# A four-layer-step decoder trunk: gate weights of three column tiles split ahead, the second half's transposes at column tiles 5 to 8, and a PSUM bank of its own for the fourth product

## The chip, the core and the metric

The kernel runs on one core of one Trainium2 chip. The metric is the device time of one launch in microseconds (us). The core has a matrix engine (PE, TensorE), which multiplies a loaded 128x128 block by a moving operand of up to 512 columns and adds into PSUM; a vector engine (DVE); a scalar engine (ACT), used here for casts, copies and SiLU; POOL (GpSimd), which does elementwise work in SBUF and issues some DMAs; and SP (SyncE), which issues most DMAs. Every engine works through its own list of instructions in a fixed order, and waits at an instruction whose semaphores are not yet there; what stands behind it waits too. PSUM has eight banks of 512 float32 values per partition.

## The reference

The trunk has DEPTH = 2 layers; each layer is a feed-forward step, a mixer, and a second feed-forward step, all on x of 1024 rows by 1024 columns in float32. Only the feed-forward step is touched here:

```
def swiglu(x, wg, wu, wd):
    return (jax.nn.silu(x @ wg) * (x @ wu)) @ wd

f = swiglu(rmsnorm(h, ffn_pre_g), ffn_w_gate, ffn_w_up, ffn_w_down)   # D_FF = 1408
h = h + 0.5 * rmsnorm(f, ffn_post_g)
```

The mixer of layer 0 is differential attention beside gated linear attention; that of layer 1 is stick-breaking attention. There are four feed-forward steps, called here by layer and step: first (layer 0, f0), second (layer 0, f1), third (layer 1, f0), fourth (layer 1, f1). The second and the fourth follow a mixer; the third follows the second directly.

## The kernel before

**Precision.** Every operand of a matrix product is split into a rounded part (a cast on ACT) and the remainder (a subtraction on DVE, L337 for weights, L277 or L280 for the others); a product is three matmuls per 128 rows of the contraction (`mm3`, L287 to L289). A *quarter* is four such blocks, 12 matmuls of 512 columns, into one PSUM bank.

**The gate and up projections** (`gu`). The 1408 columns are NF = 11 column tiles of 128. The 1024 rows of x are two halves of 512. Two loops run over the tiles. The first loop computes the first half of the gate: per tile one quarter with the first four row blocks (first quarter) and, two tiles later, one with the other four into the same bank (second quarter, `a12`), with a copy of the bank in between (L434) and SiLU at the end (L414). In the same loop the second half of x is prepared: `second_half` transposes it on PE (L327), a pair of blocks in each of four column tiles, and `combos` makes from it on DVE and ACT the sums and differences of Strassen's scheme (L388 to L397, split by L276 and L277). The second loop then does seven products' worth of work as five quarters per tile: the first three into the banks pb, pc and pd; the fourth adds to pc and the fifth to pd. DVE reads the banks in between:

```
tt(out=c22, in0=pc, in1=u2, op=ALU.add)          # L472
tt(out=c22, in0=pd, in1=c22, op=ALU.add)         # L486
self.quarter(pc, w4, A22, False, True)           # fourth product, L488
tt(out=c21, in0=pc, in1=u2, op=ALU.add)          # L489
```

Weights come by SP as `rawt` tiles of 512 KB into four buffers of pool rp, and are split into six buffers of pool wp (two quarters per gate tile, so three tiles fill the pool). The up weights are first combined with the gate's on POOL (`blocks`, L421 to L424, four instructions a tile; t2 is the output of L422).

**The down projection** (`down_strassen`) has products da, db, dc, de and dd, each into four banks, from `ph` (the output of `gu`) and from rows of the down weights or sums of them, `rawd` tiles of 256 KB. After a half is done, `epilogue` adds it to the residual stream and normalizes it for the next step: DVE (L571, L232), a power on POOL (L234, the tile rs), DVE (L575 or L580), a square on ACT (L243), L232, L234 again, and the scaling on DVE (L248). The first half's rows are transposed on PE at once (`make_x`, L268). The second half's rows (tiles fo or xn) are those that `second_half` of the next step transposes.

**Order.** The instructions of an engine are put in order by a scheduler when the program is built; what goes through `pin` (keep_in_program_order) keeps its order against other pinned instructions of its engine. In the first loop the matmuls of the first tiles and all transposes are pinned on PE. The steps in `jobs` are DMAs that POOL issues: they copy and add blocks of weights in DRAM (the tiles vsum for the mixer's value weights, wsum for its output weights, dsum for the down weights), a few per column tile. The first feed-forward step also makes the masks of the mixer on POOL in this way. Before the end of a stage, `first_weights` already loads and splits the first weights of the next.

Of the kernel before, what the change touches and what calls it, by code (L numbers as in the profile page):

```python
# [19 lines left out]
P = 128  # L20
# [69 lines left out]
class Trunk:  # L90
# [263 lines left out]
    def gu(self, cx, wg, wu, A, xn1, gname, gi, jobs, begun):  # L354
# [45 lines left out]
        pin = self.tc.keep_in_program_order  # L400
        paces = 3, -(-len(jobs[1]) // NF)

        def job(loop):
            for f in jobs[loop][:paces[loop]]:
                f()
            del jobs[loop][:paces[loop]]

# [18 lines left out]

        for c in range(NF):

            self.pin_mm = pin if c < 6 else None
            h = [self.ph.tile([P, TB], F32, name="ph%d" % tb, tag="ph") for tb in range(2)]  # L430
            w0, w1 = begun if begun and c == 0 else self.gate_weights(wg, c)
# [3 lines left out]
            while len(second) > (c < 8):  # L435
                a12()
            second.append((ps, w1, h))
            ph.append(h)
            if 2 <= c <= 5:
                second_half(c - 2)  # L440
            if 4 <= c <= 7:
                combos(c - 4)
            if c > 2:
                job(0)
# [11 lines left out]
        for c in range(NF):  # L456
# [5 lines left out]
            pd = self.acc.tile([P, TB], F32, name="pd", tag="acc")  # L462
            if c == NF - 1:
                pe = self.acc.tile([P, TB], F32, name="pe", tag="acc")
                pf = self.acc.tile([P, TB], F32, name="pf", tag="acc")
# [19 lines left out]
            else:  # L485
                tt(out=c22, in0=pd, in1=c22, op=ALU.add)  # L486
                w4, w3 = self.split_w(B["t4"]), self.split_w(B["b22"])
                self.quarter(pc, w4, A22, False, True)  # L488
                tt(out=c21, in0=pc, in1=u2, op=ALU.add)  # L489
# [7 lines left out]
            job(1)  # L497
# [113 lines left out]
    def ffn(self, l, f, x0, xn1, hsrc, hdst, last):  # L611
# [8 lines left out]
        jobs = [], []  # L620
        if l + f == 0:
            jobs = self.mask_steps() + sums((self.value_blocks(0), self.tv)), sums(down, (self.out_blocks(0), self.td))
        elif l == 0:
            jobs = [], sums(down, (self.value_blocks(1), self.tv))
        elif f == 0:
            jobs = [], sums(down)
# [4 lines left out]
        r = self.down_strassen(wd, self.wd[l, f], ph, pg, hsrc, hdst, None if last else nxt)  # L631
# [19 lines left out]
    def down_strassen(self, w, T, ph, pg, hsrc, hdst, nxt):  # L651
# [994 lines left out]
    def build(self):  # L1646
# [14 lines left out]
        for h in x1:  # L1661
# [6 lines left out]
                  (lambda l=l, f=int(step[1]): self.gate_weights(a["ffn_w_gate"][l, f], 0)) for l, step in stages]  # L1668
# [43 lines left out]
```

## Time and profile before

| | |
|---|---|
| time, median of 3 runs | 2486.64 us (2486.34 to 2493.13) |
| profiled execution | 2488.17 us, span 2486.2 us |
| mean granted TensorE clock | 0.985 |
| PE busy | 2352.8 us, 95% of the span |
| DVE, ACT, POOL busy | 1840.1, 1141.2, 723.4 us |

The span runs from the first to the last instruction of the profiled execution; 1.97 us lie around it. In a row of the timeline stand start, duration, engine, line and operation, output and inputs, the count of instructions merged into it and, in square brackets, how long the engine was idle before it and what ended the wait. In a row of the windows stand the length of the stretch and, for each engine, its busy time. Line numbers are those of the kernel before. The feed-forward steps' first loops lie at about 17 to 90 us, 937 to 1016 us, 1285 to 1359 us and 2140 to 2217 us.

### The profile page before, as it was taken

To read this page: it belongs to the slowest core of one execution; us is meant where nothing else is said; L and a number is where in the kernel's file an instruction comes from. 1 tells how busy PE (TensorE), PEld (TensorE's weight loads), DVE (VectorE), ACT (ScalarE), POOL (GpSimd) and SP (SyncE) were. 2 spreads that over 40 slices of the span, in tenths; PEclk is the share of its full clock that TensorE was granted. 3 is DMA by queue.
4 is the path that set the end of the run, shared out by engine and by line. 5 is a ranking of instruction groups with operands and counts; after the bars stand their busy time and mean duration, and the time that the engine had idled before them with its cause. 6 is when DMAs were issued, how large, how long until landed. Compare 5 with 4: busy or idle time off the path is not lost. (4 is left out here: it accounts for less than half of the span.)

```text
span 2486.2 us, 31734 instructions
## 1 busy us (share of the span) xinstructions
PE 2352.8 (95%) x11165; PEld 1925.0 (77%) x11165; DVE 1840.1 (74%) x2877; ACT 1141.2 (46%) x2285; POOL 723.4 (29%) x729
## 2 busy tenths in 40 slices
PE   7999999999888898999989999999999999799998
PEld 6778877777677776877768878778888878588886
DVE  7768789387577778678688677785767677786777
ACT  6323456332466666423456225463333345652343
POOL 3547210011011111567022563110332430234520
PEclk9999999999999998999999999999999999899999
DMA  8867444411112463767454743355574244532234
GB/s 240 229 154 187 141 148 155 143 52 68 60 60 77 150 222 108 194 151 180 140 184 125 162 118 123 122 167 180 126 185 104 90 131 163 176 85 76 73 110 170
DMA packets 278407, 343.64 MB, mean 138 GB/s; under 512 B 13972, under 2 KB 190312, under 8 KB 277736
## 3 DMA queue, kind: packets, MB, share of 16 engines
q1 hardware_dynamic: 251352, 261.39, 33.6%
q0 software_dynamic: 26896, 80.22, 14.2%
q8 instruction: 88, 1.44, 0.2%
q14 instruction: 71, 0.58, 0.1%
HBM read 292.28 MB, written 124.78 MB: 168 GB/s over the span
## 5 line engine op out<-in xcount | busy, mean ns | idle before, releaser
L234 POOL TENSOR_TENSOR rs<-ms,nhalf 128x1 f32<-128x1 f32 (+1 forms) x136 | 103.7, 769 | 839.6 <-DVE ms L232 728.7
L336 ACT CAST wq<-rawt 128x512 fp32r<-128x512 f32 x264 | 163.3, 622 | 362.6 <-PE pc L289 181.9
L337 DVE TENSOR_TENSOR wq<-rawt,wq 128x512 fp32r<-128x512 f32 x264 | 246.5, 938 | 41.9 <-ACT wq L336 37.9
L276 ACT CAST hl<-rawd 128x512 fp32r<-128x512 f32 x212 | 130.7, 620 | 212.0 <-PE dc L289 63.9
L277 DVE TENSOR_TENSOR hl<-rawd,hl 128x512 fp32r<-128x512 f32 x212 | 155.4, 737 | 81.6 <-ACT hl L276 81.5
L287 PE MATMUL pps<-hl,wh 128*128 128x512 f32 x512 | 209.3, 409 | 1.4 <-ACT k L966 1.2
L288 PE MATMUL pps<-hl,wh 128*128 128x512 f32 x512 | 203.6, 398 | 0.0
L289 PE MATMUL pps<-hl,wl 128*128 128x512 f32 x512 | 202.9, 396 | 0.0
L421 POOL TENSOR_TENSOR rawt<-rawt 128x512 f32<-128x512 f32 x44 | 65.7, 1494 | 342.7 <-DMA rawt<-in_ffn_w_up_dram 287.0
L287 PE MATMUL pa<-hl,wq 128*128 128x512 f32 x352 | 143.1, 407 | 5.8 <-ACT wq L336 3.2
L289 PE MATMUL pa<-hl,wq 128*128 128x512 f32 x352 | 141.0, 401 | 8.1 <-DVE wq L337 8.1
L287 PE MATMUL pc<-hl,wq 128*128 128x512 f32 x336 | 133.0, 396 | 12.7 <-DVE c L472 11.8
L288 PE MATMUL pa<-hl,wq 128*128 128x512 f32 x352 | 140.5, 399 | 0.0
L289 PE MATMUL pc<-hl,wq 128*128 128x512 f32 x336 | 133.3, 397 | 0.0
L288 PE MATMUL pc<-hl,wq 128*128 128x512 f32 x336 | 133.3, 397 | 0.0
L288 PE MATMUL pd<-hl,wq 128*128 128x512 f32 x336 | 131.3, 391 | 0.0
L289 PE MATMUL pd<-hl,wq 128*128 128x512 f32 x336 | 131.2, 391 | 0.0
L287 PE MATMUL pd<-hl,wq 128*128 128x512 f32 x336 | 131.1, 390 | 0.0
L1076 DVE TENSOR_TENSOR_SCAN a<-a,zero 128x128 f32<-128x128 f32 (+3 forms) x64 | 90.2, 1409 | 46.5 <-POOL a L1073 46.2
L983 PE MATMUL z<-k,q 128*128 128x512 f32 (+2 forms) x480 | 113.6, 361 | 9.5 <-ACT k L966 4.3
L287 PEld LDWEIGHTS pps<-hl,wh 128*128 128x128 f32 x512 | 97.7, 191 | 21.5 <-ACT k L966 2.6
L289 PEld LDWEIGHTS pps<-hl,wl 128*128 128x128 f32 x512 | 97.5, 191 | 21.1
(359 smaller groups left out, 6642.0 us busy)
## 6 DMA issues: line engine op xcount, KB each, us to landing
rawt<-in_ffn_w_gate_dram SPq DMA_DIRECT2D x88, 512.0 KB, 4.0
dsum<-in_ffn_w_down_dram POOLq DMA_DIRECT2D x48, 640.0 KB, 8.0
rawt<-in_ffn_w_up_dram SPq DMA_DIRECT2D x44, 512.0 KB, 4.2
rawd<-dsum SPq DMA_DIRECT2D x80, 256.0 KB, 2.7
hres<-h SPq DMA_DIRECT2D x40, 512.0 KB, 2.7
h<-hres SPq DMA_DIRECT2D x40, 512.0 KB, 4.6
rawd<-in_ffn_w_down_dram SPq DMA_DIRECT2D x76, 256.0 KB, 2.7
dsum<-dsum POOLq DMA_DIRECT2D x16, 640.0 KB, 5.7
```

The source lines that it names most:

```text
L234: nc.gpsimd.tensor_tensor(out=rs, in0=ms, in1=self.nhalf.to_broadcast([P, n]) if n > 1 else self.nhalf, op=ALU.pow)
L276: nc.scalar.copy(out=t[:, 0], in_=src)
L277: nc.vector.tensor_tensor(out=t[:, 1], in0=src, in1=t[:, 0].bitcast(F32), op=ALU.subtract)
L287: pin(nc.tensor.matmul(ps, lhsT=ah, rhs=bh, start=first, stop=False, skip_group_check=more))
L288: pin(nc.tensor.matmul(ps, lhsT=ah, rhs=bl, start=False, stop=False, skip_group_check=more))
L289: pin(nc.tensor.matmul(ps, lhsT=al, rhs=bh, start=False, stop=last, skip_group_check=more))
L336: nc.scalar.copy(out=w[:, 0], in_=src)
L337: nc.vector.tensor_tensor(out=w[:, 1], in0=src, in1=w[:, 0].bitcast(F32), op=ALU.subtract)
L421: gt(out=b11, in0=b12, in1=b11, op=ALU.subtract)
L983: nc.tensor.matmul(z[:, :wide], lhsT=lhs[:, i * P:(i + 1) * P], rhs=rhs[:, c0:c0 + wide], start=j == 0, stop=j == len(passes) - 1 and not ...
L1076: nc.vector.tensor_tensor_scan(out=ra, data0=ra, data1=self.zero1.to_broadcast([P, n]), initial=1.0, op0=ALU.mult, op1=ALU.add)
```

## The change

Four things are changed together.

1. `first_weights` loads and splits the gate weights of three column tiles instead of one before the last epilogue of the stage before.
2. In the first loop of `gu`, `second_half` is called at the column tiles 5 to 8 (c = 4 to 7) instead of 3 to 6, `combos` at 6 to 9 (c = 5 to 8) instead of 5 to 8; matmuls are pinned up to c = 7; the second quarters stay two tiles behind up to c = 8.
3. In the second loop the fourth product has a bank of its own, pe, in every tile (before: in the last alone), and a new SBUF tile c23, so that L472's and L486's results are kept apart. The numbers of instructions are the same.
4. In the first feed-forward step, POOL's mask steps and the sums vsum leave the first loop of `gu` (three steps a tile) and stand in `down_strassen`, all at once, behind POOL's last subtraction of that function (L725).

```diff
@@ gu
-        paces = 3, -(-len(jobs[1]) // NF)
-        def job(loop):
-            for f in jobs[loop][:paces[loop]]:
-                f()
-            del jobs[loop][:paces[loop]]
+        pace = -(-len(jobs) // NF)
+        def job():
+            for f in jobs[:pace]:
+                f()
+            del jobs[:pace]
...
         for c in range(NF):
-            self.pin_mm = pin if c < 6 else None
+            self.pin_mm = pin if c < 8 else None
             h = [self.ph.tile([P, TB], F32, name="ph%d" % tb, tag="ph") for tb in range(2)]
-            w0, w1 = begun if begun and c == 0 else self.gate_weights(wg, c)
+            w0, w1 = begun.pop(0) if begun else self.gate_weights(wg, c)
             ps = self.acc.tile([P, TB], F32, name="pa", tag="acc")
             self.quarter(ps, w0, A[0:4], True, True)
             nc.scalar.copy(out=h[1], in_=ps)
-            while len(second) > (c < 8):
+            while len(second) > (c < 9):
                 a12()
             second.append((ps, w1, h))
             ph.append(h)
-            if 2 <= c <= 5:
-                second_half(c - 2)
             if 4 <= c <= 7:
-                combos(c - 4)
-            if c > 2:
-                job(0)
+                second_half(c - 4)
+            if 5 <= c <= 8:
+                combos(c - 5)
...
             pd = self.acc.tile([P, TB], F32, name="pd", tag="acc")
+            pe = self.acc.tile([P, TB], F32, name="pe", tag="acc")
             if c == NF - 1:
-                pe = self.acc.tile([P, TB], F32, name="pe", tag="acc")
                 pf = self.acc.tile([P, TB], F32, name="pf", tag="acc")
...
             else:
-                tt(out=c22, in0=pd, in1=c22, op=ALU.add)
+                v = c22
+                c22 = tm.tile([P, TB], F32, name="c23", tag="c23")
+                tt(out=c22, in0=pd, in1=v, op=ALU.add)
                 w4, w3 = self.split_w(B["t4"]), self.split_w(B["b22"])
-                self.quarter(pc, w4, A22, False, True)
-                tt(out=c21, in0=pc, in1=u2, op=ALU.add)
+                self.quarter(pe, w4, A22, True, True)
+                tt(out=c21, in0=pe, in1=v, op=ALU.add)
@@ ffn
         if l + f == 0:
-            jobs = self.mask_steps() + sums((self.value_blocks(0), self.tv)), sums(down, (self.out_blocks(0), self.td))
+            jobs = sums(down, (self.out_blocks(0), self.td))
+            steps = sums((self.value_blocks(0), self.tv)) + self.mask_steps()
@@ down_strassen
         for j in range(KH):
             gt(out=ph[j + KH][0], in0=ph[j][0], in1=ph[j + KH][0], op=ALU.subtract)
+        for f in steps:
+            f()
@@ build
-                  (lambda l=l, f=int(step[1]): self.gate_weights(a["ffn_w_gate"][l, f], 0)) for l, step in stages]
+                  (lambda l=l, f=int(step[1]): [self.gate_weights(a["ffn_w_gate"][l, f], c) for c in range(3)])
+                  for l, step in stages]
```

How the built order moves is shown at three places. The first is ACT at the start of the second feed-forward step, where the first half's gate begins and the second half's last epilogue still runs. COPY ph is the copy behind a first quarter, ACTIVATE ph the SiLU behind a second quarter, `junk,ss<-h` the square of a residual row block, and `xr<-xps` reads the first transposes. Before:

```order
L434 COPY ph_8550<-pa 128x512
L336 CAST wq<-rawt 128x512
L243 ACTIVATE junk,ss<-h 128x1024
L414 ACT_TABLE_LOAD
L414 ACTIVATE ph_8509<-pa 128x512
L243 ACTIVATE junk,ss<-h 128x1024
L336 CAST wq<-rawt 128x512
L243 ACTIVATE junk,ss<-h 128x1024 x2
L329 ACTIVATE xr<-xps,gcol 128x512 x2
```

With the change:

```order
L433 COPY ph_8578<-pa 128x512
L336 CAST wq<-rawt 128x512
L243 ACTIVATE junk,ss<-h 128x1024
L412 ACT_TABLE_LOAD
L412 ACTIVATE ph_8545<-pa 128x512
L243 ACTIVATE junk,ss<-h 128x1024
L433 COPY ph_8607<-pa 128x512
L243 ACTIVATE junk,ss<-h 128x1024
L412 ACTIVATE ph_8561<-pa 128x512
L243 ACTIVATE junk,ss<-h 128x1024
```

Behind these follow three casts, the copy of the fifth tile, a cast, the third SiLU and then the first L329: the transposes now stand behind eight quarters instead of four, and the last square behind the second SiLU.

The second place is DVE between the second and the third feed-forward step, where the second half's sums (L757, L700), the weight splits (L337) and the epilogue (L571, L232, L580) stand in one list. Before:

```order
L757 TENSOR_TENSOR fo_3_11254<-dd_10862,u_10226 128x512
L700 TENSOR_TENSOR fo_2_11249<-fo_2_11249,pg 128x512
L337 TENSOR_TENSOR wq<-rawt,wq 128x512
L280 SCALAR_TENSOR_TENSOR hl<-xps,gcol,hl 128x512
L700 TENSOR_TENSOR fo_3_11254<-fo_3_11254,pg 128x512
L571 TENSOR_TENSOR s_11275<-fs_10221 128x1
```

With the change:

```order
L761 TENSOR_TENSOR fo_3_11294<-dd_10902,u_10266 128x512
L702 TENSOR_TENSOR fo_2_11289<-fo_2_11289,pg 128x512
L337 TENSOR_TENSOR wq<-rawt,wq 128x512
L280 SCALAR_TENSOR_TENSOR hl<-xps,gcol,hl 128x512
L702 TENSOR_TENSOR fo_3_11294<-fo_3_11294,pg 128x512
L337 TENSOR_TENSOR wq<-rawt,wq 128x512 x4
L571 TENSOR_TENSOR s_11331<-fs_10261 128x1
```

The splits of the second and the third tile (four) stand ahead of the epilogue; before, they stood one by one among its instructions.

The third place is POOL in the down projection of the first feed-forward step. With the change:

```order
L727 TENSOR_TENSOR ph_746<-ph_428,ph_746 128x512
L82 DMA vsum_132<-in_hyb_w_in_dram 256x512 x2
L82 DMA vsum_134<-in_hyb_w_in_dram 256x512 x2
L82 DMA vsum_132<-in_hyb_w_in_dram 256x512 x2
L82 DMA vsum_134<-in_hyb_w_in_dram 256x512 x2
L82 DMA vsum_133<-vsum_132 16x8192 x2
L82 DMA vsum_133<-in_hyb_w_in_dram 256x512 x2
L82 DMA vsum_135<-vsum_133 16x8192 x2
L82 DMA vsum_135<-in_hyb_w_in_dram 256x512 x2
L168 MEMSET zero_2427 128x1
```

After this MEMSET come 24 more mask instructions, and then the epilogue's powers (L234, 16 of them). Before, L234 stood directly behind L725, and all of these stood ahead of the first loop's and the second loop's L421 to L424.

More of the change, by code (lines that the diff above doesn't have):

```diff
@@ L399, in gu @@
         ph, second = [], []
-        pin = self.tc.keep_in_program_order
-        paces = 3, -(-len(jobs[1]) // NF)
-        def job(loop):
-            for f in jobs[loop][:paces[loop]]:
+        pace = -(-len(jobs) // NF)
+        def job():
+            for f in jobs[:pace]:
                 f()
-            del jobs[loop][:paces[loop]]
+            del jobs[:pace]
         def a12():
@@ L425, in blocks @@
             return {"t1": b11, "t2": t2, "t3": b12, "t4": b21, "b22": b22}
+        pin = self.tc.keep_in_program_order
         for c in range(NF):
-            self.pin_mm = pin if c < 6 else None
+            self.pin_mm = pin if c < 8 else None
             h = [self.ph.tile([P, TB], F32, name="ph%d" % tb, tag="ph") for tb in range(2)]
-            w0, w1 = begun if begun and c == 0 else self.gate_weights(wg, c)
+            w0, w1 = begun.pop(0) if begun else self.gate_weights(wg, c)
             ps = self.acc.tile([P, TB], F32, name="pa", tag="acc")
@@ L496, in gu @@
                 self.down_sums(ph, c - 1 - NF // 2)
-            job(1)
+            job()
         tmp.close()
@@ L619, in ffn @@
         down = self.down_blocks(l, f), self.wd[l, f]
-        jobs = [], []
+        jobs, steps = [], []
         if l + f == 0:
-            jobs = self.mask_steps() + sums((self.value_blocks(0), self.tv)), sums(down, (self.out_blocks(0), self.td))
+            jobs = sums(down, (self.out_blocks(0), self.td))
+            steps = sums((self.value_blocks(0), self.tv)) + self.mask_steps()
         elif l == 0:
-            jobs = [], sums(down, (self.value_blocks(1), self.tv))
+            jobs = sums(down, (self.value_blocks(1), self.tv))
         elif f == 0:
-            jobs = [], sums(down)
+            jobs = sums(down)
         ph = self.gu(cx, wg, wu, x0, xn1, "ffn_pre_g", 2 * l + f, jobs, self.begun_w)
@@ L630, in ffn @@
         nxt = ("mix_pre_g", l) if f == 0 else ("ffn_pre_g", 2 * (l + 1))
-        r = self.down_strassen(wd, self.wd[l, f], ph, pg, hsrc, hdst, None if last else nxt)
+        r = self.down_strassen(wd, self.wd[l, f], ph, pg, hsrc, hdst, None if last else nxt, steps)
         cx.close()
@@ L649, in down_sums, with down_strassen @@
         self.s1.append(s1)
-    def down_strassen(self, w, T, ph, pg, hsrc, hdst, nxt):
+    def down_strassen(self, w, T, ph, pg, hsrc, hdst, nxt, steps):
         nc = self.nc
```

## The prediction

> **What bounds the kernel now.** I began with the page's first part: PE is the bound, so the question is where it stands still or runs slowly.
>
> ```profile
> PE 2352.8 (95%) x11165; PEld 1925.0 (77%) x11165; DVE 1840.1 (74%) x2877; ACT 1141.2 (46%) x2285; POOL 723.4 (29%) x729
> ```
>
> Then PE's waits (who waited for whom: us, times, longest). The three largest lie in the stages that change, 36.6 us together:
>
> ```profile
> PE xps L327 <- DVE ms L232: 16.7, 6, 5.6
> PE pc L287 <- DVE c L472: 11.8, 7, 4.4
> PE pa L289 <- DVE wq L337: 8.1, 3, 5.5
> ```
>
> The windows (length, then busy us of PE, PEld, DVE, ACT, POOL, granted clock, DMA share, GB/s) of the second and third gate show a clock below 1:
>
> ```profile
> 937.00:1016.00 79.00, 68.63 (x302) 55.84 (x301) 65.06 (x103) 48.57 (x90) 22.58 (x22) 0.90 0.40 122
> 1285.00:1359.00 74.00, 67.04 (x300) 54.88 (x299) 61.69 (x101) 46.68 (x87) 20.82 (x20) 0.95 0.44 137
> ```
>
> The timeline of PE at the second gate shows why:
>
> ```profile
> 937.42 0.78 PE L287 MATMUL pa<-hl,wq 128*128 128x512 f32 x1
> ...
> 949.64 0.39 PE L289 MATMUL pa<-hl,wq 128*128 128x512 f32 x1
> 955.67 0.45 PE L327 MATMUL xps<-ident,fo 128*128 128x128 f32 x1 [5.64 <-DVE ms L232]
> ...
> 961.15 1.33 PE L327 MATMUL xps<-ident,fo 128*128 128x128 f32 x5 [1.38 <-DVE fo L248]
> 962.13 0.78 PE L287 MATMUL pa<-hl,wq 128*128 128x512 f32 x1
> 962.70 0.63 PE L288 MATMUL pa<-hl,wq 128*128 128x512 f32 x1
> 963.13 0.63 PE L289 MATMUL pa<-hl,wq 128*128 128x512 f32 x1
> ```
>
> Starts of matmuls lie 0.227 us apart at full clock (the stretch of 48 from 937.42 to the end of the row at 949.64, less its slow start and one wait of 0.65), so a quarter of 12 takes 2.72. PE does four quarters, then stands at the transposes until the second half's epilogue has scaled its rows, which comes row block by row block; behind that, starts lie 0.43 apart for nine matmuls (to 965.97), 1.8 us more than at 0.227. So what is read as one wait costs this stage 5.64 + 1.32 + 1.38 + 1.38 and the slow matmuls. DVE is busy in 65.06 of the 79 us, but with idle time before each scaling: it waits in a chain (DVE, ACT, POOL, DVE) that no engine fills.
>
> **The change, part by part.** I sum against the profiled execution, 2488.17 us (span 2486.2, 1.97 around it), which lies 1.5 above the median.
>
> *Second and fourth gate: +12.2 and +12.0.* Eight quarters now stand ahead of the transposes. The four before took 937.42 to 949.87, 12.45; four more at 2.72 end at 960.8. What PE now asks of DVE is the rows of the epilogue and two splits more, and both stand there already:
>
> ```profile
> 955.50 0.68 DVE L337 TENSOR_TENSOR wq<-rawt,wq 128x512 fp32r<-128x512 f32 x1
> ...
> 960.34 0.75 DVE L248 TENSOR_SCALAR fo<-h,rs 128x1024 f32<-128x1024 f32 x1 [0.44 <-POOL rs L234]
> ```
>
> The last rows are ready at 961.1. Six splits are done ahead; the seventh quarter needs the next, at about 955.3, and DVE's slot for it ends at 956.2: a wait of 1.0. PE so comes to the transposes at 961.8, finds all rows there, and leaves at about 962.5 where it left at 962.13, with four quarters (10.9) more behind it; the 1.8 at half clock goes as well: 10.9 − 0.4 + 1.7 = 12.2. The fourth gate has the same shape,
>
> ```profile
> 2157.90 0.45 PE L327 MATMUL xps<-ident,fo 128*128 128x128 f32 x1 [5.63 <-DVE ms L232]
> ...
> 2164.37 0.77 PE L287 MATMUL pa<-hl,wq 128*128 128x512 f32 x1
> ```
>
> and leaves at 2164.6 by the same steps: 12.0. Nothing is added to the epilogue's own list in these two stages; ACT gets two copies (L434) and a SiLU ahead of the last square, 0.6 each, which come between the rows. Bounds for each: 6 (those and the splits delay the chain by half of what PE does more) to 13 (no wait at all).
>
> *Third gate: +8.8.* Here PE waited for weight splits behind the epilogue on DVE:
>
> ```profile
> 1289.77 0.50 PE L289 MATMUL pa<-hl,wq 128*128 128x512 f32 x1 [1.51 <-DVE wq L337]
> ...
> 1298.24 0.79 PE L289 MATMUL pa<-hl,wq 128*128 128x512 f32 x1 [5.45 <-DVE wq L337]
> 1298.83 0.63 PE L287 MATMUL pa<-hl,wq 128*128 128x512 f32 x1
> ...
> 1305.93 1.04 PE L327 MATMUL xps<-ident,xn 128*128 128x128 f32 x8
> ```
>
> ```profile
> 1289.03 0.69 DVE L337 TENSOR_TENSOR wq<-rawt,wq 128x512 fp32r<-128x512 f32 x1
> ...
> 1301.31 0.75 DVE L248 TENSOR_SCALAR xn<-h,rs 128x1024 f32<-128x1024 f32 x1 [0.44 <-POOL rs L234]
> ```
>
> With the splits ahead of the epilogue the 5.45 and the slow matmuls behind it (about 2.7) go, and of the 1.51 some 0.5. Three splits at 0.6 push the epilogue back 1.9, so its last rows come at 1304.0; PE, through eight quarters, wants them at about 1308, so 4 us cover this. Bounds 4 to 10.
>
> *First gate: +1.4.* ACT's cast of t2 waited on POOL, which stood behind the vsum DMAs, and PE's banks came late:
>
> ```profile
> 81.97 0.62 ACT L336 CAST wq<-t 128x512 fp32r<-128x512 f32 x1 [6.90 <-POOL t L422]
> ```
> ```profile
> 83.13 0.50 PE L287 MATMUL pa<-hl,wq 128*128 128x512 f32 x1 [0.53 <-ACT ph L434]
> ```
>
> This and a second wait of 0.75 with their slow starts go. Bounds 0 to 1.6.
>
> *The bank of its own: +9.0.* The worst of the seven waits of L287 for L472, on PE and on DVE, and another:
>
> ```profile
> 147.11 0.76 PE L287 MATMUL pc<-hl,wq 128*128 128x512 f32 x1 [4.42 <-DVE c L472]
> ```
> ```profile
> 146.29 0.68 DVE L472 TENSOR_TENSOR c<-pc,ph 128x512 f32<-128x512 f32 x1
> ...
> 147.96 0.68 DVE L486 TENSOR_TENSOR c<-pd,c 128x512 f32<-128x512 f32 x1
> ```
> ```profile
> 1480.19 0.47 PE L287 MATMUL pc<-hl,wq 128*128 128x512 f32 x1 [1.87 <-DVE c L472]
> ...
> 1481.61 0.63 PE L289 MATMUL pc<-hl,wq 128*128 128x512 f32 x1
> ```
>
> The fourth product waits no more, but the fifth still waits for L486 to have read pd. That ends at 148.6 in the worst case; the fourth product, started at 142.5, ends at 145.3, so 3.4 of 4.42 stay. The other waits shrink by about 1 each, to 0.9 or less, and three vanish: of 12.6 in all (0.81 of it on ACT) 5.3 stay. Slow matmuls behind the 1.87 (1.7) go too: 7.3 + 1.7. Bounds 2 (every stage's DVE is as late as it was) to 14.
>
> *DVE later at the start of the second loop: −5.0.* `combos` starts 10.9 us later against PE. The room for that, in the fourth stage, between its last combination and PE's start on pb:
>
> ```profile
> 2198.20:2217.50 19.30, 19.30 (x86) 15.97 (x86) 13.00 (x13) 11.22 (x21) 12.06 (x8) 1.00 0.20 56
> ```
>
> DVE is idle for 19.3 − 13.0 = 6.3. Its splits of the last sum (L277) ended 2.0 behind PE's start on pb; they will end 2.0 + 10.9 − 6.3 = 6.6 behind it. L469 to L486 take 3.3 more: 9.9 against 10.9, when the fifth product wants pd. That is just in time, if POOL doesn't slow DVE. It can:
>
> ```profile
> 87.06 6.89 DVE L277 TENSOR_TENSOR hl<-xr,hl 128x512 fp32r<-128x512 f32 x4
> ...
> 95.07 2.49 DVE L277 TENSOR_TENSOR hl<-xr,hl 128x512 fp32r<-128x512 f32 x4
> ```
>
> ```profile
> 86.57 1.70 POOL L421 TENSOR_TENSOR rawt<-rawt 128x512 f32<-128x512 f32 x1
> ...
> 91.65 1.74 POOL L424 TENSOR_TENSOR rawt<-rawt,t 128x512 f32<-128x512 f32 x1
> ```
>
> The first four splits ran beside POOL's four instructions for one tile of blocks, the second four without: 4.4 us more. Part of that now falls on the path: I take 1.25 in each of four stages, from bounds of 0 and 3.
>
> *POOL's sums and masks in the down projection: −2.5.* Before, the masks and vsum took POOL from 27.42 to 79.3:
>
> ```profile
> 27.42 0.10 POOL L168 MEMSET zero<- 128x1 f32 x1
> ...
> 36.92 2.46 POOL L82 DMA_DIRECT2D vsum<-in_hyb_w_in_dram  x4
> ...
> 78.37 0.89 POOL L82 DMA_DIRECT2D vsum<-in_hyb_w_in_dram  x1 [0.46 <-DMA vsum<-vsum]
> ```
> ```profile
> 333.31 2.33 POOL L234 TENSOR_TENSOR rs<-ms,nhalf 128x1 f32<-128x1 f32 x3 [65.64 <-DVE ms L232]
> ```
>
> Behind L725 (ended 267.7) POOL was idle for 65.64 us; the new work takes 52, so the first L234 keeps 14 us of cover. What it can cost is DMA: rawd needs 256 KB a quarter, 96 GB/s, and while vsum ran SP's queue moved 3.67 MB in 44 us, 83 GB/s:
>
> ```profile
> q1 hardware_dynamic: 7284, 3.67, 32.1%
> ```
>
> By that row the down weights fall behind by at most 14% of 42 us, 6 us; rawd is loaded ahead, so I take 2.5, from bounds of 0 and 6.5.
>
> **Sum:** 12.2 + 12.0 + 8.8 + 1.4 + 9.0 − 5.0 − 2.5 = 35.9. 2488.2 − 35.9 = 2452.3; from the median, **2450.8 us**, given as 2451.
>
> The sum leaves about eight gaps of some 1 us on PE. The row at 1480.19 shows slow matmuls behind a gap of 1.87; if each gap that I leave cost such a 1.7, it would be 14 us and the result 2465, which the range holds. I leave it out of the sum, since behind the 1.51 at 1289.77 the matmuls run on at 0.39 and 0.23 apart. The Trainium skill ("TensorE: Matmul & The Clock Gate", Part 1) has the clock fall to half after an idle window of about 3.4 us; by that rule these gaps cost nothing, and the row at 1480.19 speaks against it as a sharp bound.
>
> **The rivals.**
>
> *The wait only moves (2474).* If the epilogue is slowed in the second to fourth gate by what DVE now does ahead of it (splits, copies of the fifth tile), each keeps 6 us and its slow matmuls, 7.7: 23 us of the gain stay out. For: DVE is busy 65.06 of 79 us there. Against: the last L248 stands at 960.34 with idle time of 0.44 before each, so DVE isn't full.
>
> *POOL stops DVE altogether (2470).* If DVE's instructions with two operands in SBUF did nothing while POOL's four run, a block would cost its whole length, 86.57 to 93.39, 6.8 and not 4.4. Two blocks, those of the first two tiles, could meet the late sums in each stage: 2.4 × 2 × 4 = 19 us more. For: one split of four took 1.7 us there, not 0.6. Against: it did end, inside the block. The Trainium skill ("SBUF — State Buffer", Who interferes with whom) states such a lock: a DVE instruction that reads two operands from SBUF shares a pair of ports with POOL, and who holds it shuts the other out. By that rule the time would be this rival's; the rows at 87.06 agree with a port that changes hands, not with one kept for a whole block.
>
> *A bank of its own does nothing (2460).* The fifth product waits for L486 as long as the fourth did for L472. For: L486 stands 1.7 behind L472 at 146.29. Against: the fourth product covers 2.7.
>
> *Slower (2500).* DVE's idle 6.3 can't be used, because the weights it idles for come when they did, and the 10.9 fall on the fifth product wholly, with slow matmuls behind it as after the 5.45 in the third gate (2.7): 13.6 a stage, 54.4 in all, against 40.9 of gains (35.9 + 5.0): 13.5 slower. It decides from 10.2 a stage. For: in the window at 2198.20 DVE's idle time ends on casts of weights by ACT, one by one. Against: the sums need no weights, so they fill that idle time wherever the order lets them stand.
>
> **How the numbers follow.** Main case 0.70: its own range is 2443 (no loss on DVE or DMA) to 2462 (3 in each stage and 6.5). The wait only moves 0.13; POOL stops DVE 0.08; the bank does nothing 0.04; slower 0.05. The range of 2442 to 2472 takes the main case and the rivals at 2470 and 2460, and leaves out those at 2474 and 2500, some 2 in 10. 0.3%, 7.5 us, is about what this kernel's measurement tells from no change: faster 0.93 (the main case and the first three rivals, less 0.02 for several bounds met at once), same 0.03 (that 0.02, and 0.01 of the last rival, where a stage costs about 10), slower 0.04 (the rest of it).
>
> **What would show it.** In the profile after: L327 in the second and fourth gate without a wait over 1 us, and granted clocks of those windows near 0.98; no wait of over 1.2 for L337 in the third; waits for L472 gone from PE's list, and pd waiting for L486 a few times, 5 us in all; at the start of second loops pd's or pe's waits of about 1 us. The first L234 of the first down projection still waits for DVE, not DVE for it. Wrong would be: L327 still waiting 5 us; a wait of PE on DVE of over 5 us near the first pd of a second loop; rawd ending PE's waits between 270 and 320 us.

## The result, and the profile after

The changed kernel takes 2454.79 us (median of 4 runs, 2452.27 to 2456.84), the kernel before 2486.49 beside it: a ratio of 0.9867 with a 95% interval of 0.9846 to 0.9888, 32 us less. Forecast were 2451 us. The sum came out within 4 us; its terms did not, as the stages show. Times below are medians, for *undo_bank* of three executions, as a fourth of it took 2587.84 us at a granted clock of 0.86. A stage here runs from the start of the first matmul on pa, pb, da or va to the next such start in PE's timeline (for the second step the first pa starts at 937.42 before and at 931.30 after). The profiled executions have spans of 2486.2 and 2454.7 us:

| stage | before | after | gain | forecast |
|---|---|---|---|---|
| first gate | 73.2 | 72.3 | 0.9 | 1.4 |
| second gate | 78.2 | 66.6 | 11.6 | 12.2 |
| third gate | 73.6 | 74.9 | −1.3 | 8.8 |
| fourth gate | 77.4 | 66.6 | 10.8 | 12.0 |
| four second loops | 623.5 | 621.2 | 2.3 | 9.0 − 5.0 |
| first down projection | 114.3 | 114.2 | 0.2 | −2.5 |
| the other three | 344.5 | 344.2 | 0.3 | 0 |
| two mixers | 1084.9 | 1078.1 | 6.8 | 0 |
| all | | | 31.5 | 35.9 |

Lines of the changed kernel are shifted a little: its L433 is L434 of before (the copy), L412 is L414 (SiLU), L419 to L422 are L421 to L424 (POOL's blocks), L469 and L485 are L472 and L486, L727 is L725.

The page's first part, and PE's waits (us in total, times, longest), of the changed kernel:

```profile
PE 2347.0 (96%) x11165; PEld 1920.8 (78%) x11165; DVE 1856.3 (76%) x2877; ACT 1137.5 (46%) x2285; POOL 725.6 (30%) x729
```
```profile
PE pa L287 <- ACT ph L433: 12.3, 7, 6.4
PE pd L287 <- DVE c L485: 9.0, 6, 3.5
...
PE pa L289 <- DVE wq L337: 1.7, 3, 1.0
```

Of the three waits that led the list before (L327 for L232, pc for L472, L337) two are gone and the third is short. Two others lead instead: a copy by ACT, which the prediction did not name, and pd for L485, which it did (with 5 us in all, not 9.0). The 12.3 for the copy are one wait of 6.4 in the third gate, one of 1.2 near the end of each of the four first loops, and two of 0.6 in the second and fourth gate.

The windows of the second, third and fourth gate after, with the columns of the prediction's windows: the clock is 1.00 where PE no longer stands, and 0.95 still in the third.

```profile
931.30:997.90 66.60, 64.50 (x296) 52.74 (x297) 62.92 (x98) 46.04 (x87) 18.23 (x18) 1.00 0.41 127
1272.10:1347.10 75.00, 66.41 (x298) 54.12 (x297) 60.79 (x97) 45.40 (x86) 19.46 (x18) 0.95 0.40 123
2119.50:2186.00 66.50, 64.39 (x296) 52.69 (x297) 62.93 (x96) 45.93 (x87) 18.50 (x16) 1.00 0.33 101
```

PE's timeline in the second gate after: eight transposes in one row, with no wait in front, and the next matmul 0.79 us later.

```profile
954.69 1.03 PE L327 MATMUL xps<-ident,fo 128*128 128x128 f32 x8
955.48 0.48 PE L287 MATMUL pa<-hl,wq 128*128 128x512 f32 x1
```

In the third gate the wait stands elsewhere. PE's timeline there, and ACT's:

```profile
1276.51 0.50 PE L289 MATMUL pa<-hl,wq 128*128 128x512 f32 x1 [1.04 <-DVE wq L337]
...
1281.41 0.39 PE L289 MATMUL pa<-hl,wq 128*128 128x512 f32 x1
1288.16 0.80 PE L287 MATMUL pa<-hl,wq 128*128 128x512 f32 x1 [6.36 <-ACT ph L433]
1288.75 0.63 PE L288 MATMUL pa<-hl,wq 128*128 128x512 f32 x1
```
```profile
1281.26 1.06 ACT L243 ACTIVATE junk<-h 128x1024 bf16<-128x1024 f32 x1 [1.51 <-DMA rawt<-in_ffn_w_gate_dram]
...
1286.49 1.06 ACT L243 ACTIVATE junk<-h 128x1024 bf16<-128x1024 f32 x1 [1.34 <-issue]
1287.45 0.19 ACT L243 ACTIVATION_READ_ACCUMULATOR junk<-h 128x1 f32 x1
1287.54 1.54 ACT L433 COPY ph<-pa 128x512 f32<-128x512 f32 x3
```

PE has done three first quarters, all that can be done without a second quarter into a used bank. The banks wait to be copied, but the three copies stand on ACT behind the last epilogue's four squares, which wait for DVE to make the rows. (The bracket at 1281.26 names a load that a square doesn't read. DVE makes the rows of that square, L580, from 1279.76, and has them at about 1281.1; those of the last square end at 1286.4.) The epilogue's chain stops PE once more, through ACT instead of through DVE's splits.

### The profile page after: what moved, and what is told of

The parts are those of the page before. It is cut to its first block, busy times and chain, and to the rows that moved or that the text cites. A ratio compares the mean times of both kernels' runs of the same rounds, so it can differ in the third digit from the quotient of the medians.

```text
span 2454.7 us, 31711 instructions
## 1 busy us (share of the span) xinstructions
PE 2347.0 (96%) x11165; PEld 1920.8 (78%) x11165; DVE 1856.3 (76%) x2877; ACT 1137.5 (46%) x2285; POOL 725.6 (30%) x729
## 4 chain that ended last, share of the span: by engine, by line
PE 56%; DVE 20%; issue 9%; DMA 6%; ACT 4%; POOL 4%; POOLq 0%; DVEq 0%; SPq 0%; ACTq 0%
DVE hl L277 3%; PE pps L287 3%; DMA rawt<-in_ffn_w_up_dram 3%; PE pps L288 3%; PE pps L289 3%; PE pd L287 2%; PE pd L288 2%; PE pd L289 2%; POOL rs L234 2%; DVE wq L337 2%; PE dc L289 2%; PE dc L287 2%; PE dc L288 2%; PE po L1120 2%; PE da L287 1%
## 5 line engine op out<-in xcount | busy, mean ns | idle before, releaser
L234 POOL TENSOR_TENSOR rs<-ms,nhalf 128x1 f32<-128x1 f32 (+1 forms) x136 | 102.3, 758 | 778.6 <-DVE ms L232 668.2
L337 DVE TENSOR_TENSOR wq<-rawt,wq 128x512 fp32r<-128x512 f32 x264 | 247.0, 941 | 32.3 <-ACT wq L336 28.5
L419 POOL TENSOR_TENSOR rawt<-rawt 128x512 f32<-128x512 f32 x44 | 66.8, 1517 | 370.5 <-DMA rawt<-in_ffn_w_up_dram 227.9
L287 PE MATMUL pa<-hl,wq 128*128 128x512 f32 x352 | 141.6, 402 | 16.1 <-ACT ph L433 12.3
L287 PE MATMUL pd<-hl,wq 128*128 128x512 f32 x336 | 133.3, 397 | 9.1 <-DVE c L485 9.0
L288 PE MATMUL pd<-hl,wq 128*128 128x512 f32 x336 | 133.3, 397 | 0.0
L289 PE MATMUL pd<-hl,wq 128*128 128x512 f32 x336 | 133.0, 396 | 0.0
L987 PE MATMUL z<-k,q 128*128 128x512 f32 (+2 forms) x480 | 114.4, 363 | 10.6 <-ACT k L970 4.3
L287 PEld LDWEIGHTS pps<-hl,wh 128*128 128x128 f32 x512 | 97.8, 191 | 21.6 <-ACT k L970 2.6
L288 PEld LDWEIGHTS pps<-hl,wh 128*128 128x128 f32 x512 | 97.4, 190 | 17.3
L277 DVE TENSOR_TENSOR hl<-ph,hl 128x512 fp32r<-128x512 f32 x112 | 106.4, 964 | 0.0
L1073 ACT ACTIVATE a<-z 128x512 f32<-128x512 f32 (+2 forms) x96 | 47.4, 494 | 118.5 <-PE z L987 113.8
```

Source lines behind the costliest of these rows:

```text
L234: nc.gpsimd.tensor_tensor(out=rs, in0=ms, in1=self.nhalf.to_broadcast([P, n]) if n > 1 else self.nhalf, op=ALU.pow)
L277: nc.vector.tensor_tensor(out=t[:, 1], in0=src, in1=t[:, 0].bitcast(F32), op=ALU.subtract)
L287: pin(nc.tensor.matmul(ps, lhsT=ah, rhs=bh, start=first, stop=False, skip_group_check=more))
L288: pin(nc.tensor.matmul(ps, lhsT=ah, rhs=bl, start=False, stop=False, skip_group_check=more))
L289: pin(nc.tensor.matmul(ps, lhsT=al, rhs=bh, start=False, stop=last, skip_group_check=more))
L337: nc.vector.tensor_tensor(out=w[:, 1], in0=src, in1=w[:, 0].bitcast(F32), op=ALU.subtract)
```

## The experiments

All are compared with runs of the kernel before on the same chip. The stages in us, one profiled execution each (G gate, L second loop, D1 first down projection, M the two mixers):

| kernel | median | G1 | L1 | D1 | G2 | L2 | G3 | L3 | G4 | L4 | M |
|---|---|---|---|---|---|---|---|---|---|---|---|
| before | 2486.5 | 73.2 | 161.2 | 114.3 | 78.2 | 154.6 | 73.6 | 156.4 | 77.4 | 151.4 | 1084.9 |
| the change | 2454.8 | 72.3 | 158.1 | 114.2 | 66.6 | 159.7 | 74.9 | 152.1 | 66.6 | 151.4 | 1078.1 |
| change_again | 2452.3 | 72.7 | 158.5 | 114.2 | 66.6 | 153.1 | 74.9 | 153.3 | 66.6 | 151.4 | 1073.8 |
| undo_half | 2461.3 | 70.7 | 153.6 | 114.2 | 76.5 | 151.6 | 73.1 | 151.6 | 76.7 | 151.4 | 1076.1 |
| undo_first | 2464.7 | 72.1 | 158.5 | 114.2 | 69.1 | 151.9 | 75.4 | 153.5 | 69.4 | 151.4 | 1082.4 |
| undo_bank | 2459.5 | 72.9 | 161.4 | 114.3 | 66.6 | 154.7 | 74.6 | 156.3 | 66.6 | 151.7 | 1079.7 |
| undo_sums | 2455.8 | 81.4 | 153.2 | 114.1 | 66.6 | 157.1 | 74.6 | 153.1 | 66.6 | 151.4 | 1076.1 |
| bank_only | 2479.2 | 76.9 | 157.9 | 114.2 | 78.3 | 151.7 | 72.5 | 151.4 | 78.5 | 151.4 | 1085.9 |
| copy_first | 2445.6 | 72.4 | 157.3 | 114.2 | 66.6 | 152.7 | 67.9 | 154.0 | 66.6 | 151.4 | 1073.6 |
| first_early | 2444.4 | 70.9 | 153.5 | 114.4 | 66.6 | 152.8 | 74.7 | 152.7 | 66.6 | 151.4 | 1076.0 |
| sums_out | 2452.2 | 71.6 | 159.5 | 114.2 | 66.6 | 154.0 | 75.4 | 153.2 | 66.7 | 151.4 | 1074.7 |
| all_three | 2439.7 | 71.1 | 154.4 | 114.2 | 66.6 | 155.2 | 67.8 | 153.2 | 66.6 | 151.4 | 1078.9 |
| no_sums | 2445.4 | 72.3 | 157.9 | 114.2 | 66.6 | 151.4 | 74.9 | 153.2 | 66.6 | 151.4 | 1073.0 |
| two | 2435.1 | 71.1 | 152.7 | 114.2 | 66.6 | 157.0 | 67.8 | 153.8 | 66.6 | 151.4 | 1073.1 |

### The change once more

> The changed kernel once more, unaltered, to see how far its stages spread from one profiled execution to the next. Theory (parts that the change does not touch differ by chance): the two mixers, 570.1 and 507.9 us in the first trace, come out within 567 to 573 and 506 to 513; the second loop of the second step, 159.7 in the first trace, lies anywhere from 152 to 160; the first loops and down projections repeat within 0.5. Time 2450 to 2457. Rival (the stages are fixed by the order of the instructions): every stage within 0.5 of the first trace.

2452.3 us, ratio 0.986 (0.9838 to 0.9882). Gates, L4 and down projections repeat within 0.5 us. The second loop of the second step comes out at 153.1 where it was 159.7, the mixers at 1073.8 where they were 1078.1, a little below the range given for the first of them (566.7 against 567). So a difference in L2 of some 6 us, or in the mixers of some 4, between two single traces shows nothing, while the gates can be read to a few tenths. The rival falls.

### Each part undone

The transposes and combos back to the old tiles:

```diff
-            self.pin_mm = pin if c < 8 else None
+            self.pin_mm = pin if c < 6 else None
-            while len(second) > (c < 9):
+            while len(second) > (c < 8):
-            if 4 <= c <= 7:
-                second_half(c - 4)
-            if 5 <= c <= 8:
-                combos(c - 5)
+            if 2 <= c <= 5:
+                second_half(c - 2)
+            if 4 <= c <= 7:
+                combos(c - 4)
```

> The changed kernel with its second part undone: second_half at tiles 3 to 6, combos at 5 to 8, second quarters as before; the three tiles of weights ahead, the own bank and POOL's moved steps stay. Theory (the stage is where the gain lies): in the second and fourth gate PE again reaches the transposes after four quarters and waits for the epilogue's rows, about 10 us and slow matmuls in each, so 11 + 11 us of the gain go: 2455 + 22 = 2477, range 2472 to 2482, with L327 waiting 5.6 for L232 twice. The third gate keeps its new wait of 6.4 for the copy (L433). Second loops get up to 5 us better, as combos end 10.9 us earlier against PE: then 2472. Rival (the weights ahead alone bring the gain, since PE would otherwise wait for splits): 2455 to 2460.

2461.3 us, ratio 0.9894 (0.9874 to 0.9914): below the range that was expected. PE's waits in this kernel:

```profile
PE xps L327 <- DVE ms L232: 16.7, 6, 5.6
...
PE pd L287 <- DVE c L485: 1.4, 3, 0.6
```

The wait at the transposes is back whole, and G2 and G4 lose 20.0 us, for 22 in the theory. But the second loops gain: 153.6 + 151.6 + 151.6 + 151.4 = 608.2, against 621.2 in the first trace of the change and 616.3 in its second. The later place of the combos thus costs 8 to 13 us in the loops, and some 3 more in the first and third gate (70.7 and 73.1 against 72.3 and 74.9), of the 20 that it brings.

Weights of one tile ahead instead of three:

```diff
-                  (... [self.gate_weights(a["ffn_w_gate"][l, f], c) for c in range(3)])
+                  (... [self.gate_weights(a["ffn_w_gate"][l, f], c) for c in range(1)])
```

> The changed kernel with its first part undone: weights of one tile ahead instead of three. Theory: with the transposes at tiles 5 to 8 PE needs four quarters more of weights whose splits stand behind or among the epilogue's instructions on DVE, so the second and fourth gate each get waits for L337 of 3 to 8 us; the third gate has its old waits (1.5 + 5.5 and slow matmuls, about 10 in all) where it has 1.0 + 6.4 now, so no change there. Sum 2455 + 6 to 16 = 2461 to 2471. Rival (the shift of the transposes alone does it; splits slip in between the rows in time): 2455, with no wait of over 1.5 for L337 in the second and fourth gate.

2464.7 us, ratio 0.9909 (0.988 to 0.9938), inside the theory's range. G2 and G4 lose 2.5 and 2.8, with waits for L337, the third has its old waits, and one line came back that nobody had spoken of:

```profile
PE pa L289 <- DVE wq L337: 12.4, 4, 5.5
...
PE xps L268 <- DVE hl L280: 5.4, 2, 3.1
```

L268 are the first half's transposes, at the end of a mixer. They wait 5.4 us here and 5.4 before, and 0.7 in the change. ACT and then PE at that place (the first mixer's end) before:

```profile
932.26 0.62 ACT L336 CAST wq<-rawt 128x512 fp32r<-128x512 f32 x1 [0.62 <-DMA rawt<-in_ffn_w_gate_dram]
932.78 3.00 ACT L279 ACTIVATE hl<-xps,gcol 128x512 fp32r<-128x512 f32 x5
```
```profile
930.06 1.91 PE L268 MATMUL xps<-ident,fo 128*128 128x128 f32 x16
934.32 3.45 PE L268 MATMUL xps<-ident,fo 128*128 128x128 f32 x16 [2.35 <-DVE hl L280]
```

And after:

```profile
925.92 1.31 ACT L336 CAST wq<-rawt 128x512 fp32r<-128x512 f32 x2 [1.11 <-PE od L289]
927.13 4.90 ACT L279 ACTIVATE hl<-xps,gcol 128x512 fp32r<-128x512 f32 x8
```
```profile
926.41 1.91 PE L268 MATMUL xps<-ident,fo 128*128 128x128 f32 x16
928.67 2.63 PE L268 MATMUL xps<-ident,fo 128*128 128x128 f32 x16 [0.36 <-DVE hl L280]
```

Before, the weights' casts stood ahead of the reads of the transposes on ACT and waited for their DMA till 932.26; the transposes' banks were read late and PE's second 16 waited. With three tiles ahead the loads are issued earlier (SP issues three by 917.98, 8.4 us ahead of the first transposes; before, one at 911.64 and the next from 924.86, 5.2 ahead) and the casts that stand there find their data. From 930.06 to 937.42 before, 926.41 to 931.30 after: 2.5 us, and 3.2 at the second mixer's end (8.1 and 4.9 from the first transpose to the first pa). That is 5.7 of the 6.8 us that the mixers gained.

The fourth product back into pc:

```diff
...
-                self.quarter(pe, w4, A22, True, True)
-                tt(out=c21, in0=pe, in1=v, op=ALU.add)
+                self.quarter(pc, w4, A22, False, True)
+                tt(out=c21, in0=pc, in1=u2, op=ALU.add)
```

> The changed kernel with its third part undone: the fourth product adds to pc, as before. Theory: each of the six waits of pd for L485 (9.0 us, 3.5 at most) becomes a wait of pc for L472 that is about 1 longer, and two or three shorter ones appear, with slow matmuls behind more of them: 7 to 10 us slower, 2462 to 2465. Rival (the bank does nothing, the fifth product waits as long): 2455, waits for L472 of 9 us in all.

2459.5 us, ratio 0.9882 (0.9853 to 0.9911). The loops sum to 624.1 against 621.2 and 616.3 in the two traces of the change, and the old wait is back:

```profile
PE pc L287 <- DVE c L469: 10.6, 8, 3.6
```

By the medians that is 4.7 above the change's first comparison and 7.2 above its second, below the theory's 2462 to 2465, and the intervals overlap (that of the change reaches 0.9888). The loops alone lose 2.8 and 7.8. So a gain of the bank inside the change is seen in the returned wait, and its size, 3 to 8 us, is not shown clear of chance.

POOL's masks and vsum back into the first gate:

```diff
...
-            steps = sums((self.value_blocks(0), self.tv)) + self.mask_steps()
+            jobs = self.mask_steps() + sums((self.value_blocks(0), self.tv)), sums(...)
```

> The changed kernel with its fourth part undone: masks and vsum stand in the first loop of the first feed-forward step again, three steps a tile, not in the down projection. Theory: the first gate loses about 1 us (waits for copies behind a cast of t2), the first down projection stays at 114.2 us, as its DMAs cost nothing there: 2456. Rival (the down projection pays for the sums 2.5 us or more): 2452 or less, and a first down projection of 111.7 or less.

2455.8 us, ratio 0.9873 (0.9852 to 0.9894): no difference from the change. The down projection didn't move (114.1 and 114.2), so the sums cost nothing there. But G1 is 9.1 longer, not 1, and L1 4.9 shorter, 4.2 in all by these traces. The rows of PE, ACT and POOL at the first gate's end:

```profile
92.71 0.79 PE L287 MATMUL pa<-hl,wq 128*128 128x512 f32 x1 [7.58 <-ACT ph L433]
```
```profile
84.53 0.62 ACT L336 CAST wq<-t 128x512 fp32r<-128x512 f32 x1 [9.66 <-POOL t L420]
```
```profile
80.92 0.89 POOL L82 DMA_DIRECT2D vsum<-in_hyb_w_in_dram  x1 [1.84 <-DMA vsum<-vsum]
81.53 1.60 POOL L419 TENSOR_TENSOR rawt<-rawt 128x512 f32<-128x512 f32 x1
83.20 1.29 POOL L420 TENSOR_TENSOR t<-rawt 128x512 f32<-128x512 f32 x1
```

POOL's DMAs, which wait for each other, hold up L420; the cast of its output holds ACT; and a copy that PE needs stands behind the cast. It is the stall that the prediction found before (0.53 and 0.75 together), six times as long. Before, the copy came right behind the cast (82.50 behind 81.97). Here the cast at 84.53 also holds DVE, and ACT stops once more, at a cast of one of the sums of `combos`, until DVE has made it beside POOL:

```profile
85.19 1.10 DVE L337 TENSOR_TENSOR wq<-t,wq 128x512 fp32r<-128x512 f32 x1 [9.11 <-ACT wq L336]
86.20 1.75 DVE L394 TENSOR_TENSOR s<-s,hl 128x512 f32<-128x512 f32 x1
```
```profile
87.99 0.62 ACT L276 CAST hl<-s 128x512 fp32r<-128x512 f32 x1 [2.83 <-DVE s L394]
```

The copy comes at 92.06. In this order ACT's copy stands behind a cast of the sums that the second part moved later. That suggests that the fourth part is worth more with the second than it would have been to the kernel before; no run has the fourth part alone.

### The bank alone

```diff
+            pe = self.acc.tile([P, TB], F32, name="pe", tag="acc")
...
-                self.quarter(pc, w4, A22, False, True)
+                self.quarter(pe, w4, A22, True, True)
```

> The kernel before with the third part alone: a bank of its own for the fourth product in every tile, and c23. Theory (with the combos at their old place DVE is early, and the bank takes nearly all of the second loops' waits): second loops from 161.2, 154.6, 156.4 and 151.4 to about 154, 152, 152 and 151.4, 14 us less, time 2488 to 2474; the first loops as before. Rival (the bank gives what the prediction gave it, 9): 2479. Rival (nothing): 2488.

2479.2 us, ratio 0.9966 (0.9953 to 0.9979). The loops go from 623.5 to 612.4, 11.1 less; L2 and L3 stand at 151.7 and 151.4, where the fourth, without any wait, has always been. What is left of seven waits are two:

```profile
PE pd L287 <- DVE c L488: 4.0, 2, 2.6
```

3.7 us of it are lost in the first gate (76.9 against 73.2), where one wait for ACT's copy is 2.8 long instead of 0.8. The sum hits the rival's number. In the loops 11.1 lies between the rival's 9 and the theory's 14: the second and third came out as the theory has them (152 each), the first did not (157.9 for 154).

### Three repairs

Copies ahead of squares, in the third gate alone:

```diff
-            nc.scalar.copy(out=h[1], in_=ps)
+            copy = nc.scalar.copy(out=h[1], in_=ps)
+            # third gate, c < 3: an order edge, square c behind this copy
...
```

The comment stands for the code: an order edge fixes the order of two instructions without a wait for data.

> The changed kernel, where in the third gate ACT's copies of the first three tiles (L433) are ordered ahead of the last epilogue's squares (L243), the k-th copy ahead of the k-th square; all other orders as they are. Theory (PE stands 6.36 us at 1288 because ACT, in its order, is held by squares whose rows the epilogue hasn't made, while the bank to be copied has been ready since 1275): the wait for L433 goes, with the slow matmuls behind it; a wait of up to 1 for a split of the fourth tile may stay; third gate 74.9 to about 67.5, time 2455 to 2447. Rival (the epilogue's rows or the splits behind them set the pace, and the copy is only the last to be seen): a wait for L337 or at the transposes takes its place, third gate above 72, time 2453 to 2455.

2445.6 us, ratio 0.9829 (0.9808 to 0.985); G3 67.9 where 67.5 was expected. ACT, and PE:

```profile
1272.77 0.58 ACT L433 COPY ph<-pa 128x512 f32<-128x512 f32 x1
1273.24 1.06 ACT L243 ACTIVATE junk<-h 128x1024 bf16<-128x1024 f32 x1
```
```profile
1273.40 0.50 PE L287 MATMUL pa<-hl,wq 128*128 128x512 f32 x1 [1.19 <-ACT ph L433]
```

6.36 became 1.19 and the slow matmuls are gone; no other wait came up. So ACT's order is the cause of the 6.36 and of the third gate's loss.

The first step's transposes and combos at the old tiles, the other three steps as changed:

```diff
+        early = 0 if gi else 2
-            if 4 <= c <= 7:
+            if 4 <= c + early <= 7:
...
```

> The changed kernel with second_half and combos at the old tiles (3 to 6 and 5 to 8) in the first feed-forward step alone. Theory (nothing is waited for at the transposes of the first step, so the later place only makes DVE late in its second loop): first gate and second loop together from 230.3 to 224.4 as with the second part undone everywhere, the other three steps as in the changed kernel, time 2449. Rival (that gain came of another step, or of chance): 229 to 231, time 2455.

2444.4 us, ratio 0.9828 (0.9811 to 0.9846). G1 + L1 is 224.4, as expected to the tenth, 6.0 less: in the first step nothing waits at the transposes, and the later place is pure loss.

The second step's vsum out of its second loop:

```diff
-            jobs = sums(down, (self.value_blocks(1), self.tv))
+            jobs, steps = sums(down), sums((self.value_blocks(1), self.tv))
```

> The changed kernel, where in the second feed-forward step the sums vsum for the next layer's mixer leave the second loop for the down projection, as the first step's did; the second loop keeps the 16 steps of dsum, two a tile. Theory (the second loop's waits come of these DMAs: they hold up the up weights, POOL's blocks then come late and in pairs, and DVE beside them is slow): second loop of the second step from 159.7 to about 152.5, its down projection unchanged within 0.5, time 2448. Rival (the waits come of DVE being later by the 10.9 us of the moved combos, whatever the DMAs do): second loop at 157 or more, time 2452 to 2455.

2452.2 us, ratio 0.9859 (0.9843 to 0.9876); L2 154.0, between the two numbers, and inside what the same loop shows unaltered (152.7 to 159.7). It decides nothing about L2. One miss stands beside it: the second step's down projection, expected unchanged within 0.5, took 112.7 against 114.5, without the wait of 1.8 that PE has there on da for ACT (L714) in both traces of the change.

All three, and then the first two:

> The three edits of copy_first, sums_out and first_early together on the changed kernel. Theory (three separate places, each with its own cause): the gains add up, 7.5 + 7 + 6 = 20.5, time about 2434, range 2430 to 2439. Rival (what one stage gives is lost in the next, or waits only move on): 2442 or more.

> The edits of copy_first and first_early together on the changed kernel, without that of sums_out. Theory (sums_out's edit is worth nothing clear, the other two add up): 9.2 + 10.4 below the changed kernel by the medians, less by the stages (7.1 + 6), so 2437 to 2441. Rival (all three are needed for 2440): 2444 or more.

2439.7 us (0.9806, 0.9792 to 0.9821) and 2435.1 us (0.9788, 0.9771 to 0.9806). The first lies between its two expectations, the second 2 us below its theory's range: copy_first and first_early add up, and sums_out's edit brings nothing beside them. *two* is faster than both kernels: 2.1% (1.9 to 2.3) less than the kernel before, whose median beside it was 2488.6, and 17 to 20 us below the change's two medians.

### What makes the second loop late

> The changed kernel, where the second feed-forward step issues no DMA sums at all in its second loop: its down projection reads the first step's dsum, and the next mixer the first mixer's vsum, so these products are of other weights; the engines' instructions stay the same. Theory (the up weights land late because POOL's copies and sums in DRAM share the DMA engines): the second loop of the second step comes to 151.4 to 152, as in the fourth step, which has none, with no wait of pd for L485 in it. Rival (DVE's late combos alone): 153 to 160 as in the other traces.

```diff
-            jobs = sums(down, (self.value_blocks(1), self.tv))
+            self.wd[l, f] = self.wd[0, 0]
```

L2 is 151.36, the fourth step's 151.36 to the hundredth, with no wait for L485. The change's first trace has this, on POOL, DVE and PE:

```profile
1012.69 1.30 POOL L419 TENSOR_TENSOR rawt<-rawt 128x512 f32<-128x512 f32 x1 [9.95 <-DVE c L492]
...
1019.99 1.71 POOL L419 TENSOR_TENSOR rawt<-rawt 128x512 f32<-128x512 f32 x1
```
```profile
1016.03 1.12 DVE L337 TENSOR_TENSOR wq<-t,wq 128x512 fp32r<-128x512 f32 x1 [3.48 <-ACT wq L336]
1017.07 1.79 DVE L493 TENSOR_TENSOR ph<-ph,c 128x512 f32<-128x512 f32 x1
1018.78 1.77 DVE L494 TENSOR_TENSOR ph<-c,c 128x512 f32<-128x512 f32 x1
...
1023.87 0.68 DVE L485 TENSOR_TENSOR c<-pd,c 128x512 f32<-128x512 f32 x1
```
```profile
1024.69 0.47 PE L287 MATMUL pd<-hl,wq 128*128 128x512 f32 x1 [1.83 <-DVE c L485]
```

POOL's block comes late. The cast of its output t on ACT (1015.38) waits for POOL, the split of t on DVE waits 3.48 for the cast, and DVE's next two instructions on SBUF take 1.79 and 1.77, beside POOL's last instruction of the block and the three DMAs that it issues before the next block; 0.68 is what they take in no_sums. So L485 is late. The up weights, which POOL needs first, take these times to land (the DMA issues of the change's trace from 997 to 1047 us, and of no_sums from 990 to 1040; count, size, median us):

```profile
rawt<-in_ffn_w_up_dram SPq DMA_DIRECT2D x4, 512.0 KB, 10.8
```
```profile
rawt<-in_ffn_w_up_dram SPq DMA_DIRECT2D x4, 512.0 KB, 4.3
```

In the change's second trace, whose L2 is 153.1, it is 4.9. Read in the same way (the first 50 us of the loop), the loop is longer the later these weights land, in the ten traces that have the moved combos and the bank of its own: 151.4 at 4.3 (no_sums), 151.9 to 153.1 at 4.9 to 7.0 (four traces), 154.0 and 155.2 at 8.0 and 7.9, and 157.0 to 159.7 at 10.4 to 10.8 (three). Late up weights alone don't do it: in undo_half and bank_only, with the combos at their old place, the loop takes 151.6 and 151.7 at 8.5 and 8.6. So the loop's remaining waits need both the late combos and up weights that the DMA sums have delayed, and they vary as that delay does. The wait put down to L492 at 1012.69 is probably one for the up weights: issued at 1001.70, they land 10.8 later, at 1012.5, and L419 reads nothing that L492 writes; but L492 ends at 1012.55, so the times alone don't decide it. How much of no_sums' gain is the traffic and how much POOL's issuing of it was not separated.

## Why the prediction was right, and which steps failed

**The second and fourth gate** went by the prediction's own steps: 11.6 and 10.8 for 12.2 and 12.0, transposes without a wait, clock 1.00. Each has a wait of 1.2 for ACT's copy near its end (995.03 in the second gate) that the forecast doesn't have, about what is short.

**The third gate** is the step that failed, +8.8 forecast and −1.3 measured. "With the splits ahead of the epilogue the 5.45 and the slow matmuls behind it go" was right about DVE (L337 waits 1.04, and about 1.0 was named) and read only DVE's list. The same epilogue's squares also stand in ACT's list, ahead of the copies that free PE's next step. copy_first shows it: 7.1 of the missing 10.1 us come back when only that order is altered. The third gate is then 5.8 shorter than before; two waits of 1.19 for ACT's copy, at 1273.40 and 1327.47, that it did not have before make up 2.4 of the 3.0 that still lack. It is the rival "the wait only moves", in one stage of three and through another engine.

**The second loops** net 2.3 in the first trace and 7.2 in the second, for 9.0 − 5.0. Both terms were too small: alone, the bank takes 11.1 out of the loops, where 9.0 were forecast and 2 to 14 bounded (with the late combos, by undo_bank, 3 to 8); the combos' later place costs 8 to 13, where 5.0 were taken and 0 to 12 bounded. Not 1.25 in each stage, though: nothing in the fourth, most in the first two. The price was worked from the fourth step's idle time on DVE and spread over four; the fourth is the one without DMA sums. The bound of DVE's slowing beside POOL was the right row, the cause of its timing in the second step (late up weights) was not seen.

**The first gate** 0.9 for 1.4, and **the first down projection** 0.2 for −2.5. The vsum chain did run there as foreseen, and the mask steps ended ahead of the first power:

```profile
317.90 0.76 POOL L187 TENSOR_SCALAR_AFFINE_SELECT lm<-lm 128x64 f32<-128x64 f32 x1
329.02 2.86 POOL L234 TENSOR_TENSOR rs<-ms,nhalf 128x1 f32<-128x1 f32 x3 [10.36 <-DVE ms L232]
```

10.4 us of cover are left of the 14 counted, and no wait of PE on rawd came. That the down weights would fall behind, the term of −2.5, is a step that failed: D1 is 114.1 to 114.4 in every run, with the sums and without.

**The mixers** stood at zero in the sum and gave 6.8, of which 5.7 is the change's (undo_first brings it back) and the rest within what two traces of one kernel differ by. That the first tiles' loads are issued at the end of the mixer, on queues and engines that still work for it, was written down as a part of the change and priced nowhere.

That the total was within 4 us is therefore luck in good part: −10 in the third gate, some −2 in the loops and −2 in the other gates met +6.8 in the mixers and +2.7 in the down projection. Of the rivals, POOL stopping DVE altogether didn't come: beside POOL's blocks DVE's instructions took 1.75 to 1.79 and went on. "By that rule the time would be this rival's" follows only if DVE were shut out over a whole block of four; the instructions ended one by one inside it, as the prediction's own rows at 87.06 show. Own banks did something, and the slower case has no support: the combos' later place cost the worst loop 8.1 us (159.7 against 151.6 in undo_half) and the four together 13 at most, where that case needs 10.2 in each.

## What to carry to other kernels

When a wait is taken away by putting work ahead of a slow chain, read the list of every engine that holds a link of that chain, not only of the engine named in the wait: here DVE's part of the epilogue was passed and ACT's was not. Moving a step later is paid by whoever uses its output; it paid where PE stood idle for that step's input and was a loss of 6 us where it didn't. And before a single stage is compared between two traces, it is worth one run to see which stages repeat: the gates did to tenths, a loop beside DMA traffic differed by 6.7 us.

## What was not expected of the hardware

Short gaps can slow PE, but their length alone doesn't decide it. In the change's first trace, after the 1.83 us at 1024.69, matmuls run on at full pace for 1.5 us and then at half:

```profile
1025.93 0.47 PE L289 MATMUL pd<-hl,wq 128*128 128x512 f32 x1
1026.20 0.63 PE L287 MATMUL pd<-hl,wq 128*128 128x512 f32 x1
...
1028.76 0.63 PE L287 MATMUL pb<-hl,wq 128*128 128x512 f32 x1
```

The starts go from 0.23 to 0.43 apart, and this gap of 1.83 costs 1.3 us more on pd and 0.4 on pb; another of 1.83 at 1055.93 costs 1.7 on pd. Behind 1.04 (at 1276.51) and 1.19 (in copy_first) there is none. That is the row at 1480.19 of before again. But in the same trace of before, PE goes on at full pace behind a gap of 1.85:

```profile
100.11 0.47 PE L287 MATMUL pc<-hl,wq 128*128 128x512 f32 x1 [1.85 <-DVE c L472]
100.42 0.39 PE L288 MATMUL pc<-hl,wq 128*128 128x512 f32 x1
```

So it does behind 2.69 at 949.00 in undo_first and 3.04 at 1059.27 in undo_sums. Counted over all 14 traces, for waits of 0.9 us and more on the banks of the gates, second loops and down projections (behind the first 30 us): none up to 1.78 is followed by a slow stretch, 11 of the 23 from 1.81 to 3.04 are, and all from 3.23 are. One place shows it best, the start of the second down projection, where PE waits 1.8 to 1.9 on da in nine of the traces: slow matmuls follow in undo_half, undo_bank and first_early and make that stage 116.1 to 116.7 long, and none follow in the other six, where it is 114.5 to 114.7. What decides was not found. The slow ones at 1.83 and 1.87 lie below the idle window of about 3.4 us that the Trainium skill ("TensorE: Matmul & The Clock Gate", Part 1) names; where the slow stretch comes, about half the price of such a wait is behind it.
